# Seven products of quarters in place of the seventh product of blocks

## The chip, the cores and the metric

The kernel runs on one core of a Trainium2 chip. A core has a matrix engine (TensorE, PE in the profile; its weight loads are listed apart as PEld), two engines that work element by element (VectorE, DVE, and ScalarE, ACT), GpSimd (POOL), which here issues the DMAs that convert types, and SyncE (SP), which issues the other DMAs. Each engine works through its own instructions in order and waits at semaphores for the others. The metric is the time of one execution in microseconds (us), as the device measures it.

## The reference

The kernel computes a matrix product with a leaky ReLU behind it, all in 32-bit floats outside:

```python
m, k, n = 4096, 4096, 4096        # a: m x k, b: k x n, standard normal entries; alpha = 0.01
x = np.matmul(a, b)
return np.where(x > 0, x, alpha * x)
```

## The kernel before

**Blocks.** `out` is cut into 16 regions of 1024 rows by 1024 columns, (g, j) for row group g and column group j. The sum over k is cut into four units u of 1024 (eight slices of 128 each). Inputs are converted to 16-bit floats by the loading DMA. In a region, a is a 2x2 matrix of blocks (512 rows by 2048 of k), and so is b (2048 of k by 512 columns): b11 and b12 are units 0 and 1 with the left and the right columns, b21 and b22 units 2 and 3. Each block is held as two tiles k = 0, 1, one per unit. The pool of b (L73) has two buffers for each of the tags b11, b12, b21, b22, that is one block each: the next region's block goes where this region's block was, as soon as the last reader is done.

**Regions.** Region (0, 0) is computed directly, with 512 matmuls. The other 15 use Winograd's form of Strassen's scheme: seven products of blocks instead of eight, 64 matmuls of 128x128 weights by 512 columns each. `regions` (L480) has the order: (0,1) to (0,3), then for g = 1, 3 the columns 2, 0, 1, 3, and for g = 2 the columns 2, 0, 3, 1. The first of a group computes the sums of a's blocks (`sum_a`, named s1 to s4). The last of a group is called turning: while it runs, the next group's a is loaded by POOL through three buffers (`a16_pool`) and transposed by DVE (`fetch_a`, L660). The very last region, (3, 3), is called final. Column 2 is kept converted in DRAM, and regions (g, 2) load it through SP; all others load b through POOL.

**The seven products** (`PRODUCTS`, `product`, L617): 0 is a11*b11, 1 a12*b21, 2 s2*b11, 3 s3*b12, 4 s1*b11, 5 a22*b21, 6 s4*b22. The blocks of b are changed in place between them by DVE (`b_sum`): behind product 0, b12 becomes b22-b12 and b11 becomes b11+b12; behind product 1, b21 becomes b21-b11; behind product 2, b11 becomes b22-b11 with what b11 and b22 then are. b22 itself is product 6's operand. Products 0, 2, 4 and 6 accumulate in four PSUM banks y, products 1, and then 3 and 5, in the four others, z; the next region changes the two sets.

**Leaving.** `keep` copies the four banks to SBUF with ACT (u1 behind product 0, u2 behind product 2, v behind product 3). `add` adds banks onto such a copy with DVE, and `leave` applies the leaky ReLU with DVE and stores with SP. After product 6 the banks are copied, passed through the ReLU and stored (L748 to L754).

**The order.** The schedule is that of the program, written by hand: each engine executes its instructions in the order of the code. In a region's code the next region's blocks are fetched like this: b12 behind product 3 (L707), b11 behind product 4 (L728), b21 behind product 5 (L733), b22 behind product 6 (L747). A block is two units, a unit two DMAs of 512 KB on POOL's queue.

**Measuring.** The kernel sums squares of every block of a and b, and from these judges at the end (`judge`, L566) whether the scheme's result stands; otherwise a direct product follows (L757). One measure (`Measure`, L207): three squares by ACT (`begin`), one DVE addition, which frees a buffer for the fourth square, the fourth square, two more additions and a fold of some six small DVE instructions (`end`). `MEASURED` (L594) says which blocks are measured in which region and where: `middle` begins behind product 0, ahead of the copies of u1 on ACT, and ends behind the first b sums; the first of `late_ones` begins behind product 2 ahead of the copies of u2, the further ones behind product 3; `fifth` and `sixth` measure blocks that have been loaded for the next region.

Of the kernel before, what the change touches and what calls it, by code (L numbers as in the profile page):

```python
# [8 lines left out]
P = 128  # L9
DT = mybir.dt.float16  # L10
# [14 lines left out]
KC = 8  # L25
# [14 lines left out]
GREATEST = 1e8  # L40
# [4 lines left out]
def kernel(  # L45
# [6 lines left out]
):  # L52

# [20 lines left out]
    c_pool = ctx.enter_context(tc.tile_pool(name="c", bufs=8))  # L74
# [132 lines left out]
    class Measure:  # L207
# [21 lines left out]
        def end(self):  # L229
            total, *more = self.held  # L230
            nc.vector.tensor_add(total, total, more[0])  # L231
            self.square(3)
            nc.vector.tensor_add(total, total, more[1])  # L233
            nc.vector.tensor_add(total, total, self.held[3])  # L234
            fold(self.which, total, self.place(2), self.pairs)

# [246 lines left out]
    def fetch_b(i, quads):  # L483

        if i >= len(regions):
            return
        for half, nt in quads:
            for u in (2 * half, 2 * half + 1):
                fetch_unit(i, u, nt)
# [65 lines left out]
    def measure(i, which, x, y, room=None):  # L555

        if which:
            tiles = [have_b[i, 2 * x + k, y] for k in range(2)]
        else:
            tiles = [at[regions[i][0], x, 2 * y + k] for k in range(2)]  # L560
        parts = halves(tiles[0]) + halves(tiles[1])
        if tiles[0] is first_a:
            return MeasureFirst(which, parts, None)
        return Measure(which, parts, not which, room)

    def judge():  # L566
# [29 lines left out]
        (1, 2): (None, [A11], B12, B11), (1, 0): (B21, [B22, A12], B12, B11),  # L596
        (1, 1): (B21, [B22, A22], None, None),
        (2, 2): (None, [A11], None, None), (2, 0): (None, [A12], B12, B11),
        (2, 3): (B21, [B22, A22], None, None),
        (3, 2): (None, [A11], None, None), (3, 0): (A12, [A22], None, None),  # L600
    }

    PRODUCTS = [("a11", 0, 0), ("a12", 1, 0), ("s2", 0, 0), ("s3", 0, 1), ("s1", 0, 0), ("a22", 1, 0), ("s4", 1, 1)]

# [5 lines left out]
    for i, (g, j) in enumerate(regions):  # L610
# [19 lines left out]
        def keep(banks):  # L630
            kept = []
            for mt in range(MT):
                t = c_pool.tile([P, NT], FP32, name="c", tag="c")
                nc.scalar.copy(t, banks[mt])  # L634
                kept.append(t)
            return kept
# [34 lines left out]
        first_of_group = i == 0 or regions[i - 1][0] != g  # L671

# [3 lines left out]
        u1 = keep(y)  # L676
# [19 lines left out]
        u2 = keep(y)  # L696
# [9 lines left out]
        v = keep(z)  # L706
        fetch_b(i + 1, [(0, 1)])  # L707
        fetch_a(1, 0)
        for m in late_ones[1:]:
            m.begin()  # L710
            m.end()

        product(4, y, False)
        a21 = None
        if turning:
            new_s(g + 1, "s1")
            t = new_s(g + 1, "s2").rearrange("p k c m e -> p (k c m e)").bitcast(BF16)
            a21 = measure(i + 1, 0, 1, 0, t.rearrange("p (n w) -> p n w", n=4))
            a21.begin()
        add(v, y)  # L720
        leave(v, 1, 1)
        if a21:
            a21.end()
# [22 lines left out]
        product(6, y, False)  # L746
        fetch_b(i + 1, [(1, 1)])  # L747
        if final:  # L748
            even = nc.values_load(good[0:1, 0:1], min_val=0, max_val=1)
        for mt in range(MT):  # L750
            t = c_pool.tile([P, NT], FP32, name="c", tag="c")
            nc.scalar.copy(t, y[mt])  # L752
            leaky(t)
            nc.sync.dma_start(place(g, 0, mt, j, 1), t)  # L754


    with tc.If(even == 0):  # L757
        for m in range(M // RM):
# [9 lines left out]
            for n in range(N // NT):  # L768
# [12 lines left out]
                for mt in range(MT):  # L781
                    t = c_pool.tile([P, NT], FP32, name="c", tag="c")
                    nc.scalar.copy(t, banks[mt])
                    leaky(t)
                    nc.sync.dma_start(out[(m * MT + mt) * P:(m * MT + mt + 1) * P, cols], t)
# [35 lines left out]
```

## Time and profile before

| what | value |
| --- | --- |
| time, median of 3 runs | 1582.35 us (1581.85 to 1582.39) |
| the profiled execution, its own time | 1582.06 us |
| span of its instructions | 1580.2 us |
| granted TensorE clock, mean | 0.999 |
| PE busy | 1569.9 us (99%) |
| DVE busy | 956.8 us (61%) |
| ACT busy | 371.9 us (24%) |
| POOL busy | 306.5 us (19%) |
| casting DMA queue (POOL) | 141.59 MB, 60.2% of 16 engines' span |
| other DMA queue (SP) | 104.49 MB, 18.1% |

Times are microseconds, those of single instructions nanoseconds where marked ns. A line of the timeline has the start, the length, the engine, the line in the code, the operation with what it writes and reads, its shape and count, and in brackets the idle time before it with what ended that. A line of stages has the stretch from the span's start, its length, each engine's busy time with its count of instructions, then the granted clock, the DMA share and GB/s. A busy PE is not one at its peak, since matmuls overlap: what counts is the distance between their starts. A DMA share can be over 1, because the packets of an engine overlap.

### The profile page before, as it was taken

Reading aid. Unit: us, or ns where it says so; the run is one execution under the profiler, and the core shown is the slowest. Engines: PE = TensorE matmul, PEld = TensorE weight load, DVE = VectorE, ACT = ScalarE, POOL = GpSimd, SP = SyncE. Lnnn points to the kernel's source line nnn. Section 1 sums busy time; section 2 is a strip of 40 time slices with the busy share of each in tenths; the row PEclk is TensorE's granted clock in tenths of the full one; section 3 lists DMA queues with packets and bytes.
Section 4 is the critical chain, followed back from the end, with each engine's and each line's share of the span. In section 5 each row is a group of like instructions: output and inputs, shape, how many; then the busy total and the mean of one; then the engine's idle time right before and its main releaser. Section 6 shows DMA issues by size and latency. Waiting matters only on the chain.

```text
span 1580.2 us, 18237 instructions
## 1 busy us (share of the span) xinstructions
PE 1569.9 (99%) x7275; PEld 711.0 (45%) x7275; DVE 956.8 (61%) x1046; ACT 371.9 (24%) x390; POOL 306.5 (19%) x482
## 2 busy tenths in 40 slices
PE   9999999999999999999999999999999999999998
PEld 4444444444444444444444444444444444444443
DVE  4378758576876767647776464763878546351433
ACT  2201243302223364301221024431022122000110
POOL 5641110144002011124201102012520110201100
PEclk9999999999999999999999999999999999999999
DMA  9998795999539287499935919569993783938702
GB/s 244 187 215 180 161 281 144 198 189 210 203 72 204 72 146 148 82 215 163 268 124 103 217 32 181 134 89 225 169 256 114 111 183 65 201 80 142 152 27 83
DMA packets 216514, 247.74 MB, mean 157 GB/s; under 512 B 41057, under 2 KB 178529, under 8 KB 212322
## 3 DMA queue, kind: packets, MB, share of 16 engines
q0 software_dynamic: 173952, 141.59, 60.2%
q1 hardware_dynamic: 42178, 104.49, 18.1%
q8 instruction: 59, 0.97, 0.2%
q10 hardware_dynamic: 288, 0.39, 0.1%
q14 instruction: 37, 0.30, 0.1%
HBM read 310.38 MB, written 75.50 MB: 244 GB/s over the span
## 4 chain that ended last, share of the span: by engine, by line
PE 94%; DMA 4%; DVE 1%; issue 0%; POOL 0%; ACT 0%; SPq 0%; DVEq 0%
PE ps L625 92%; PE ps L274 2%; DMA b<-in_b_dram 2%; DMA a<-in_a_dram 1%; DVE a L136 1%; DMA a_in<-in_a_dram 0%; DVE part L313 0%; POOL a L127 0%; DVE part L309 0%; POOL b L184 0%; PE turned L361 0%; DVE a L368 0%; DVE c L302 0%; ACT c L752 0%; ACT a L368 0%
## 5 line engine op out<-in xcount | busy, mean ns | idle before, releaser
L625 PE MATMUL ps<-b,a 128*128 128x512 f16 x3840 | 836.1, 379 | 0.0
L625 PE MATMUL ps<-b,s 128*128 128x512 f16 x2880 | 628.9, 379 | 0.0
L625 PEld LDWEIGHTS <-a 128*128 128x128 f16 x3840 | 375.7, 98 | 453.1
L625 PEld LDWEIGHTS <-s 128*128 128x128 f16 x2880 | 281.8, 98 | 339.8
L500 POOL DMA_DIRECT2D b<-in_b_dram x184 | 136.7, 749 | 971.1 <-PE ps L625 646.9
L553 DVE TENSOR_TENSOR b<-b 128x4096 f16<-128x4096 f16 x112 | 253.4, 2290 | 100.9 <-DMA b<-in_b_dram 69.7
L640 DVE TENSOR_TENSOR c<-ps,c 128x512 f32<-128x512 f32 x180 | 111.7, 683 | 266.0 <-PE ps L625 189.5
L634 ACT COPY c<-ps 128x512 f32<-128x512 f32 x180 | 92.7, 600 | 607.4 <-PE ps L625 597.1
L302 DVE SCALAR_TENSOR_TENSOR c<-c 128x512 f32<-128x512 f32 x240 | 149.5, 686 | 77.3 <-ACT c L752 77.3
L127 POOL DMA_DIRECT2D a<-in_a_dram x252 | 143.9, 578 | 174.6 <-DVE a L136 103.5
L136 DVE STREAM_TRANSPOSE a<-a 128x512 uint32<-128x512 uint32 (+2 forms) x96 | 115.7, 1246 | 88.0 <-DMA a<-in_a_dram 87.9
L222 ACT ACTIVATE sq<-b 128x2048 bf16<-128x2048 f16 x64 | 119.4, 1913 | 107.0 <-DVE sq L231 93.1
L752 ACT COPY c<-ps 128x512 f32<-128x512 f32 x60 | 31.1, 600 | 364.6 <-PE ps L625 364.6
L274 PE MATMUL ps<-b,a 128*128 128x512 f16 x512 | 112.8, 379 | 1.8 <-DVE part L313 0.9
L222 ACT ACTIVATE sq<-a 128x2048 bf16<-128x2048 f16 x48 | 88.9, 1925 | 62.9 <-DVE sq L231 48.7
L274 PEld LDWEIGHTS <-a 128*128 128x128 f16 x512 | 49.6, 98 | 62.8 <-issue 3.1
L231 DVE TENSOR_TENSOR sq<-sq 128x2048 bf16<-128x2048 bf16 x27 | 33.0, 1222 | 32.2 <-ACT sq L222 32.2
L234 DVE TENSOR_TENSOR sq<-sq 128x2048 bf16<-128x2048 bf16 x27 | 33.1, 1225 | 17.2 <-ACT sq L222 17.2
L233 DVE TENSOR_TENSOR sq<-sq 128x2048 bf16<-128x2048 bf16 x27 | 33.1, 1226 | 4.7 <-ACT sq L222 2.3
L222 ACT ACTIVATE s<-a 128x2048 bf16<-128x2048 f16 x12 | 22.5, 1918 | 20.9 <-DVE a L136 20.9
L184 POOL DMA_DIRECT2D b<-in_b_dram x32 | 22.9, 726 | 6.1 <-DMA b<-in_b_dram 2.5
L240 DVE TENSOR_TENSOR sq<-sq 128x1024 bf16<-128x1024 bf16 x29 | 20.1, 692 | 1.0
(64 smaller groups left out, 256.2 us busy)
## 6 DMA issues: line engine op xcount, KB each, us to landing
b<-in_b_dram POOLq DMA_DIRECT2D x192, 512.0 KB, 8.3
out_dram<-c SPq DMA_DIRECT2D x240, 256.0 KB, 6.9
a<-in_a_dram POOLq DMA_DIRECT2D x244, 128.0 KB, 5.5
b<-kept SPq DMA_DIRECT2D x24, 1024.0 KB, 7.8
kept<-b SPq DMA_DIRECT2D x8, 1024.0 KB, 8.0
b<-in_b_dram POOLq DMA_DIRECT2D x24, 256.0 KB, 9.1
b_in<-in_b_dram SPq DMA_DIRECT2D x7, 512.0 KB, 7.7
out_dram<-part SPq DMA_DIRECT2D x4, 512.0 KB, 6.6
```

Of the source, the lines that this page charges most:

```text
L127: nc.gpsimd.dma_start(a16[32 * q:32 * q + 32], src.rearrange("(g i) w -> i g w", i=32))
L136: nc.vector.transpose(part.rearrange("p c m e -> p c (m e)").bitcast(U32) .rearrange("p c (g i) -> p g c i", i=32), src[:, :, i * n:(i + 1 ...
L222: nc.scalar.activation(to, self.parts[n], SQUARE)
L233: nc.vector.tensor_add(total, total, more[1])
L234: nc.vector.tensor_add(total, total, self.held[3])
L274: nc.tensor.matmul(ps, a_cols(at[0, h, u], c, mt, (h, u) == (0, 0)), bt[0, u, nt][:, c, :], start=first, stop=last,)
L302: nc.vector.scalar_tensor_tensor(t, t, alpha, t, op0=MULT, op1=MAX if alpha <= 1 else MIN)
L500: nc.gpsimd.dma_start(t[:, c:c + 4, :], b_rows(j, u, c, 4, nt))
L553: nc.vector.tensor_tensor(f(to), f(x0), f(x1), op)
L625: nc.tensor.matmul(banks[mt], a_cols(t, c, mt, t is first_a), B(half, nt, k)[:, c, :], start=first and (k, c) == (0, 0), stop=(k, c) == (1 ...
L634: nc.scalar.copy(t, banks[mt])
L640: nc.vector.tensor_add(acc[mt], banks[mt], acc[mt])
```

## The change

In nine regions (groups 1 to 3, neither turning nor final) product 6 is made by `quarters_product`. s4 and b22 are cut into 2x2 quarters (256 rows by 1024 of k, 1024 of k by 256 columns), and seven products of quarters replace the one product: 16 matmuls of 128 weights by 256 columns each, 112 in all. Four of them accumulate partly onto the banks y of product 4, the others in two banks that product 5 used. ACT copies and DVE additions combine them, and the sum with y leaves through `leave`.

The sums of s4's quarters (`sums_s4`) are made once a group, in its first region, and kept in DRAM (`kept_s`, 2 MB, four SP stores); the two other regions load them by SP behind product 4. The sums of b22's quarters (`sums_b`, four DVE instructions) are made in each of the nine regions. Their room is b12's two buffers and the three buffers of `a16_pool` (`rooms`). So b12 of the next region can't be loaded behind product 3 there: the four units of b22 and b12 are fetched behind the products of quarters, in the order in which their buffers come free.

b12 and b11 of the next region are then no longer measured ahead in the regions (1,2), (1,0) and (2,0). Instead `MeasureApart` reads the blocks of b once more, converted, into the measure's buffers by POOL, and squares them there: two such measures in (2,0), one in (3,0), three in (3,1). The copies for leaving become pairs of tiles with two tags c0 and c1 instead of one tag with eight buffers. The judge's upper limit is 1e7 instead of 1e8.

```diff
-    c_pool = ctx.enter_context(tc.tile_pool(name="c", bufs=8))
+    c_pool = ctx.enter_context(tc.tile_pool(name="c", bufs=2))
...
+    class MeasureApart(Measure):
+        def square(self, n):
+            to = self.place(n)
+            half, nt, jb = self.parts
+            nc.gpsimd.dma_start(
+                to.bitcast(DT).rearrange("p (c n) -> p c n", n=NT),
+                b_rows(jb, 2 * half + n // 2, n % 2 * 4, 4, nt))
+            nc.scalar.activation(to, to.bitcast(DT), SQUARE)
+            self.held.append(to)
...
-        (1, 2): (None, [A11], B12, B11), (1, 0): (B21, [B22, A12], B12, B11),
+        (1, 2): (None, [A11], None, None), (1, 0): (B21, [B22, A12], None, None),
         (1, 1): (B21, [B22, A22], None, None),
-        (2, 2): (None, [A11], None, None), (2, 0): (None, [A12], B12, B11),
+        (2, 2): (None, [A11], None, None), (2, 0): (B12 + (0,), [A12, B11 + (0,)], None, None),
         (2, 3): (B21, [B22, A22], None, None),
-        (3, 2): (None, [A11], None, None), (3, 0): (A12, [A22], None, None),
+        (3, 2): (None, [A11], None, None), (3, 0): (A12, [A22, B12 + (1,)], None, None),
+        (3, 1): (B11 + (1,), [B12 + (3,), B11 + (3,)], None, None),
...
+    def rooms(i):
+        two = [b_pool.tile([P, 2, KC * HALF], DT, name="q", tag="b12") for _ in range(2)]
+        three = [a16_pool.tile([P, KC * HALF], DT, name="sq4", tag="a16") for _ in range(3)]
+        tq = {2: two[0][:, 0], 1: two[0][:, 1], 4: two[1][:, 0]}
+        sq = {1: three[0], 2: three[1], 3: three[2], 4: two[1][:, 1]}
+        return tq, sq
...
+    def sums_b(i, tq):
+        y = quarters_b(i)
+        f = lambda n: tq[n].rearrange("p (c n) -> p c n", n=HALF)
+        tt = nc.vector.tensor_tensor
+        tt(y[0, 1], y[1, 1], y[0, 1], SUB)
+        tt(f(2), y[0, 1], y[0, 0], ADD)
+        tt(f(1), y[1, 1], f(2), SUB)
+        tt(f(4), y[1, 0], f(2), SUB)
+    def sums_s4(g, sq):
...
+        tt(f(1), x[1, 0], x[1, 1], ADD)
+        tt(f(2), f(1), x[0, 0], SUB)
+        tt(f(3), x[0, 0], x[1, 0], SUB)
+        tt(f(4), x[0, 1], f(2), SUB)
+        for n in range(4):
+            nc.sync.dma_start(kept_s[n], sq[n + 1])
...
+        def quarters_product(i, y, acc, other, tq, sq):
...
+            def part(xq, yq, to, first=False):
+                for c in range(KC):
+                    for m in range(2):
+                        rows = slice(m * P, (m + 1) * P)
+                        nc.tensor.matmul(
+                            to[m], xq[:, c // 2, rows, c % 2], yq[:, c, :],
+                            start=first and (c, m) == (0, 0), stop=c == KC - 1, skip_group_check=True,
+                        )
+            part(x[0, 1], b[1, 0], onto(0, 0))
+            part(x[0, 0], b[0, 0], into(acc), True)
+            nc.scalar.copy(block(0, 0), pair(acc))
+            part(quarter_a(sq[4]), b[1, 1], onto(0, 1))
+            part(quarter_a(sq[2]), f(2), into(acc))
+            nc.scalar.copy(block(0, 1), pair(acc))
+            part(quarter_a(sq[1]), f(1), into(other), True)
+            nc.vector.tensor_add(block(0, 1), pair(other), block(0, 1))
+            part(quarter_a(sq[3]), b[0, 1], into(acc))
+            for n in (1, 0):
+                nc.scalar.copy(block(1, n), pair(acc))
+            nc.vector.tensor_add(block(1, 1), pair(other), block(1, 1))
+            part(x[1, 1], f(4), onto(1, 0))
+            for mt in range(MT):
+                nc.vector.tensor_add(kept[mt], y[mt], kept[mt])
             return kept
...
+        in_quarters = g > 0 and not turning and not final
...
         product(3, z, True)
-        v = keep(z)
-        fetch_b(i + 1, [(0, 1)])
+        v = keep(z, side)
+        if not in_quarters:
+            fetch_b(i + 1, [(0, 1)])
         fetch_a(1, 0)
         for m in late_ones[1:]:
             m.begin()
             m.end()
+        if in_quarters:
+            tq, sq = rooms(i)
+            if first_of_group:
+                sums_s4(g, sq)
+                sums_b(i, tq)
         product(4, y, False)
...
         add(v, y)
         leave(v, 1, 1)
+        if in_quarters and not first_of_group:
+            for n in (4, 2, 1, 3):
+                nc.sync.dma_start(sq[n], kept_s[n - 1])
+            sums_b(i, tq)
...
-        product(6, y, False)
-        fetch_b(i + 1, [(1, 1)])
...
+        if in_quarters:
+            kept_c = quarters_product(i, y, new_bank(zbank + 2), new_bank(zbank + 3), tq, sq)
+            for u, nt in ((3, 1), (0, 1), (2, 1), (1, 1)):
+                fetch_unit(i + 1, u, nt)
+            leave(kept_c, 0, 1)
+            side = 1 - side
+        else:
+            product(6, y, False)
+            fetch_b(i + 1, [(1, 1)])
```

## The prediction

> R is the start of a region's product 0, T the start of its product 6; times behind them are us. A unit is half of a block of b (1 MB, two DMAs of 512 KB).
>
> **What bounds the kernel now.** I read the chain first.
>
> ```profile
> 122.86 1450.41 PE ps L625 x6720
> ```
>
> After 122.86 us it is matmuls alone: 215.8 ns each, 13.81 us a product, 96.7 us a region. A matmul saved there is time saved, and a wait put in is time lost. The PE timeline gives the pace of other widths and of a cold start:
>
> ```profile
> 1.19 4.88 PE L100 MATMUL wp<-w 128*128 128x512 f16 x11 [1.19 <-DVE x L86]
> ...
> 12.47 0.64 PE L361 MATMUL turned<-ident,a_rounded 128*128 128x128 f16 x8
> ...
> 689.05 13.98 PE L625 MATMUL ps<-b,s 128*128 128x512 f16 x64
> 702.86 27.79 PE L625 MATMUL ps<-b,a 128*128 128x512 f16 x128
> ```
>
> Eight of 128 columns, each with its own weights, take 0.64 us with the last one's 0.22 us: 60 ns apart. Next, stages (the last columns are granted clock, DMA share and GB/s): casting loads of b alone, two products before a region's end, and the end of the run.
>
> ```profile
> 112.00:122.00 10.00, 10.00 (x48) 4.48 (x47) 8.18 (x13) 0.00 (x0) 0.74 (x1) 1.00 1.24 206
> 689.05:702.86 13.81, 13.81 (x65) 6.27 (x64) 4.44 (x8) 0.45 (x1) 2.96 (x4) 1.00 1.17 226
> 1575.00:1577.00 2.00, 0.00 (x0) 0.00 (x0) 0.00 (x0) 0.00 (x0) 0.00 (x0) 1.00 0.38 139
> 1577.00:1578.00 1.00, 0.00 (x0) 0.00 (x0) 0.00 (x0) 0.00 (x0) 0.00 (x0) 0.51 0.03 8
> ```
>
> Backlogged casting loads move 206 GB/s, 5.1 us a unit, and around a region's end the DMA engines are already full. Last, DVE in the turning region (1,3), R = 702.86:
>
> ```profile
> 708.30 4.69 DVE L553 TENSOR_TENSOR b<-b 128x4096 f16<-128x4096 f16 x2 [2.77 <-DMA b<-in_b_dram]
> 716.39 4.69 DVE L553 TENSOR_TENSOR b<-b 128x4096 f16<-128x4096 f16 x2 [3.40 <-DMA b<-in_b_dram]
> 721.00 2.37 DVE L136 STREAM_TRANSPOSE a<-a 128x1024 uint32<-128x1024 uint32 x2
> ...
> 750.35 2.10 DVE L136 STREAM_TRANSPOSE a<-a 128x512 uint32<-128x512 uint32 x2 [3.75 <-DMA a<-in_a_dram]
> 752.37 4.45 DVE L553 TENSOR_TENSOR b<-b 128x4096 f16<-128x4096 f16 x2
> ```
>
> The first b sums wait for b22, with b12 long there. The last line makes product 4's operand: its first half is ready at 754.6, product 4 starts at 758.1. So there are 3.5 us of slack, and 2.9 in the next turning region, (2,1) (1141.9 against 1144.9). Durations come from the groups of the page and the list by line:
>
> ```profile
> L361 PEld LDWEIGHTS <-a_rounded 128*128 128x128 f16 x32 | 2.5, 120 | 2.4 <-DVE a_rounded L345 1.6 <-issue 0.6
> L640 DVE TENSOR_TENSOR c<-ps,c 128x512 f32<-128x512 f32 x180 | 111.7, 683 | 266.0 <-PE ps L625 189.5 <-issue 76.5
> L231 DVE TENSOR_TENSOR sq<-sq 128x2048 bf16<-128x2048 bf16 x27 | 33.0, 1222 | 32.2 <-ACT sq L222 32.2
> L222 ACT ACTIVATE sq<-b 128x2048 bf16<-128x2048 f16 x64 | 119.4, 1913 | 107.0 <-DVE sq L231 93.1 <-DVE sq L234 11.6 <-DMA b<-in_b_dram 2.3
> ```
>
> Their idle columns show the chain inside a measure (ACT's fourth square waits for DVE's first addition), which the change makes longer.
>
> **What PE gains.** Removed: 64 matmuls, 13.81 us. Added: 112 of 256 columns. Between 60 ns (128) and 215.8 ns (512) a line gives 112 ns; half of 215.8 is 108. I take 110: 12.3 us, a gain of 1.5 a region, 13.4 in nine (11.5 to 15.4).
>
> **Inside the product.** Part 2 (T+1.8) needs the third z bank, which the third of four additions L640 (2.48 us for four, from T-0.4) frees at T+1.4; the fourth is needed at T+7. ACT's copies (0.5 to 0.6 us) lie beside a 1.76 us part each. The last copies and the addition from the other bank end near T+12.1; the next product 0 wants these banks at T+12.7. Cost 0, if DVE is on time. The four sums of b's quarters are 128x2048 in 16 bits, as L231's 1.22 us: 4.9 us (9.2 if the strides cost the full rate of 2.3). They stand between product 4's leaving (its additions and leaky, 2.5 us each) and product 5's additions: done at T-4, 4 us of slack. The s4 sums (4.9 us, three times) end by R+69, before product 4 does: 0. The kept loads (2 MB, SP, issued T-8 behind v's stores, landing in some 7.8 us as the kept b did, sq4 first, wanted at T+3.5): 0, at most 2 in each of six regions. On SP, u2's stores stand behind these loads; u2's place is wanted only at the next R+14: 0.
>
> **What b12's move costs.** Before, b12 was loaded during products 3 and 4, at one unit per 6.9 us. Now four units go out when the seventh product's parts 3, 5, 6 and 7 are done, on POOL's queue behind b21, and the engines share with the kept loads and 2 MB of stores. Before, the second half of b22 was summed at R+13.5; two units more of 5.1 us put it at R+24, the first half, whole with the third unit, near R+19 (kept loads could add 0 to 5). The sums (4.6 us a half) end at R+24 and R+29; product 2 needs the halves at R+27.6 and R+34.5. In ordinary regions this fits, and the DVE work behind it is done before it is wanted (quarter sums at R+79, product 5's additions at R+83).
> It doesn't in the two turning regions that follow quarters, (1,3) and (2,1). Behind the b sums DVE has a's transposes, product 1's additions, the b21 sums, eight more transposes, then product 4's operand; POOL's a loads are queued behind b12 too, so their waits (1.4, 2.6, 3.8 us) move along. A shift of 10.3 less 3.5 and 2.9: PE waits 6.8 and 7.4 at product 4. **+14.2** (0 if the a waits close, 24 with the kept loads' 5).
>
> **What the moved measuring costs.** A measure that reads b again issues three POOL DMAs, then ACT squares (1.91 us each), a DVE addition that frees a buffer, a fourth DMA (5.4 us to land, the least among b's issues), a square, an addition and 2.7 us of folding. DVE waits through the fourth read, some 7 us that a measure on the chip doesn't have.
> (3,0), one late re-read: b sums end R+29.6; the middle measure of a on the chip takes 7.4 (1.2+1.9+1.2+3.0 folding), product 1's additions and leaky 5, four b sums 9.2, the first late measure 7.4: R+58.6. Buffers come free from R+55.6, the reads land R+61 to R+66, two squares and the addition R+66.8, the fourth read R+72.3, square, addition, fold R+78.2. Then product 4's additions and leaky 5, the quarter sums 4.9, the third z addition 1.9: R+90.0, where part 2 wants that bank at R+84.7: **5.4**.
> (2,0): its middle reads are behind b12: b whole at R+21 (5.1 a unit and 2.6 per MB of stores, added up from T) to R+24 (as above), the last read 7.7 later, its square 1.9, the first copy of u1, which stands behind the squares on ACT, 0.6: R+31 to R+34. Product 2 writes that bank at R+27.6: a wait of 3.6 to 6.6; I take 4, the rows for single durations being nearer. Late, as in (3,0): 5.4. **9.4**.
> (3,1): middle the same 4; two late re-reads, the second ending some 9 us later than (3,0)'s against a T 4 later: 10.5. **14.5**.
> The next region's b11 loads stand behind the re-reads on POOL and go out near R+70 to R+77 instead of R+63; they are wanted 20 us later: 0. Taken away are the fifth and sixth measures of (1,2), (1,0), (2,0), some 11 us of DVE each: beside PE before, worth 0. Together +29.3; below: 0, if the reads land 7 us sooner; above: 12 more, if the quarter sums cost 9.2.
>
> **The clock.** It was granted in full until 1577, 3.7 us after the last matmul (1573.3), then 0.51; and the first eleven matmuls took 425 ns apart, half speed for 4.9 us. Three of the waits (6.8, 7.4, 10.5) are longer than 3.7: 0 to 2.4 us each; I take 5 in all, towards the upper end because they exceed 3.7 clearly. The Trainium skill ("TensorE: Matmul & The Clock Gate", Part 1) states that an idle window of some 3.4 us halves the clock; the trace's end agrees, and no row of before shows a gap inside the run.
>
> **Sum**, against the profiled run's 1582.06 (span 1580.2; the median of runs is 1582.35, 0.3 above): -13.4 +14.2 +29.3 +5 = +35: 1617.
>
> **Rivals.**
> Earlier landing (other side): if DMA absorbs the two units in idle time and b12 is complete at R+17 instead of R+24, turning regions don't wait, (2,0) and (3,0) don't, (3,1) keeps 3.5: 1582.1-13.4+3.5 = 1572. It decides at about R+19, where the waits sum to 13.4. For it: DMA is nearly idle from R+14 to R+41, and share above 1 counts overlapping packets. Against: 206 and 226 GB/s at the very place. 0.20.
> Only the measured regions wait, because a's transposes catch up: 1582.1-13.4+29.3+2 = 1600; 0.11. Only the turning ones, the measures being ready in time: 1582.1-13.4+14.2+3 = 1586; 0.07.
> Weight loads set the pace of narrow matmuls. For it: the row of the transposes has 120 ns for a load, more than 110. Against: those loads overlapped, as 60 ns apart shows. At 120 ns the seventh product takes 13.4 us, the gain is 3.3 in all: 1617+10 = 1627; from 123 ns on nothing is gained. 0.06. The Trainium skill (same page, Back-to-back issue gap) speaks for it: a stream of pairs of weight load and matmul is paced by both, about 81 ns at 128 columns against 56 for a matmul alone. The trace's 60 ns disagrees. With the page's 25 ns on top, an estimate for 256 columns is 134 ns, and the sum would be 1641.
> Quarter sums at the full 2.3 us each: the three late regions wait 4 more: 1617+12 = 1629; 0.05.
> The change does not do what it says: if the lowered limit 1e7 sent the work to the other path, the time would be far off; sums of some 1000 squares of standard normals stay near 1000. Under 0.01.
>
> **Numbers.** The likeliest has 0.51; its own range is 1600 to 1631. Range 1571 to 1631: it leaves out somewhat under half of the earlier-landing case and what lies above the sum (longer waits with the kept loads' 5). 0.2% is 3.2 us, about what can be told from none. Faster 0.20 (earlier landing); same 0.04 (the turning-only case reaches it in half of its width); slower 0.76.
>
> **What would show it.** Matmuls of 128x256 about 110 ns apart; PE idle ahead of product 4 in (1,3) and (2,1), ended by a DVE b sum; ahead of product 2 in (2,0) and (3,1), ended by an ACT copy behind squares; ahead of part 2 in (2,0), (3,0), (3,1), ended by DVE's additions; granted clock below 1 behind the longest; b sums starting near R+19 and R+24. Wrong would be: b sums at R+17 or before, a spacing over 123 ns, or PE without gaps.

## The result and the profile after

| | before | after |
| --- | --- | --- |
| time, median | 1582.1 us (1581.25 to 1582.39) | 1654.57 us (1652.07 to 1655.53) |
| the profiled execution / its span | 1582.06 / 1580.2 us | 1655.53 / 1653.6 us |
| granted TensorE clock, mean | 0.999 | 0.978 |

The ratio is 1.0457 (95%: 1.0438 to 1.0475): 72.5 us slower. The prediction was 1617, 35 slower, with the range 1571 to 1631. The sign was right, and the time lies above the range.

The view that says most is the list of PE's waits of the changed kernel (who waits, at which line, for whom; us in all, times, longest). These are the six largest groups that belong to the regions (two of 0.2 us for kept sums are left out); before, the chain of matmuls had none there.

```profile
PE ps L714 <- DVE c L738: 19.7, 5, 8.4
PE ps L683 <- ACT c L696: 15.6, 2, 8.4
PE ps L683 <- DVE b L566: 15.5, 5, 7.7
PE ps L683 <- ACT c L868: 5.0, 2, 3.2
PE ps L683 <- DVE c L738: 3.1, 5, 2.2
...
PE ps L683 <- DMA a<-in_a_dram: 1.4, 1, 1.4
```

L714 is the matmuls of quarters, L683 those of blocks, L738 the additions of `add`, L696 the copies of `keep`, L566 the sums of b, L868 the copies behind an undivided product 6. The same waits in the PE timeline show their places, and what stands in the regions between them:

```profile
237.19 1.07 PE L683 MATMUL ps<-b,a 128*128 128x512 f16 x2 [3.23 <-ACT c L868]
240.05 15.24 PE L683 MATMUL ps<-b,a 128*128 128x512 f16 x62 [1.79 <-ACT c L868]
...
503.76 3.66 PE L714 MATMUL ps<-b,s 128*128 128x256 f16 x32
...
774.10 16.56 PE L683 MATMUL ps<-b,s 128*128 128x512 f16 x64 [6.48 <-DVE b L566]
...
948.29 16.59 PE L683 MATMUL ps<-b,s 128*128 128x512 f16 x64 [7.27 <-ACT c L696]
...
1011.79 3.39 PE L714 MATMUL ps<-b,s 128*128 128x256 f16 x16 [3.73 <-DVE c L738]
...
1187.91 16.16 PE L683 MATMUL ps<-b,s 128*128 128x512 f16 x64 [7.71 <-DVE b L566]
...
1418.13 3.31 PE L714 MATMUL ps<-b,s 128*128 128x256 f16 x16 [6.70 <-DVE c L738]
...
1467.38 16.45 PE L683 MATMUL ps<-b,s 128*128 128x512 f16 x64 [8.36 <-ACT c L696]
...
1536.57 3.57 PE L714 MATMUL ps<-b,s 128*128 128x256 f16 x16 [8.39 <-DVE c L738]
```

Two things are to be seen. The line at 503.76 is parts 1 and 2 of a product of quarters in a region without waits: 32 matmuls in 3.66 us. And the lines behind a wait are long themselves. A product of 64 matmuls takes 13.98 us by such a line before, 13.81 from start to start; the four that follow waits of 6.5 to 8.4 us take 16.2 to 16.6, and a part of 16, 1.9 us by such a line elsewhere, takes 3.3 to 3.6. So a wait costs more than its own length. The stages of the same kernel (stretch, length, busy PE, PEld, DVE, ACT and POOL, then granted clock, DMA share, GB/s), behind two of these waits:

```profile
948.00:958.00 10.00, 9.71 (x33) 3.65 (x33) 4.63 (x8) 6.13 (x7) 0.00 (x0) 0.73 0.35 52
1536.00:1545.00 9.00, 8.18 (x54) 5.79 (x54) 3.52 (x6) 1.17 (x2) 1.48 (x2) 0.75 1.11 325
```

PE is busy nearly throughout the first of them, at a mean clock of 0.73, and makes 33 matmuls, where 10 us at 215.8 ns hold 46. Before, the clock stood at 1.00 from the first region to the end.

From the starts of the products in the two PE timelines each region's length follows. A region takes 96.7 us without quarters, and with quarters 95.1 where nothing waits ((1,2), (1,0), (2,2), (2,3), (3,2)). What the others take beyond that is split here into the waits, which the lists give, and the rest, which is matmuls made more slowly. (A wait is counted from the end of a matmul, 379 ns behind its start, and without it the next start would come after 215.8; so some 0.16 us of each of the 22 waits, 3.6 us in all, is in the last column.)

| region | length | beyond 96.7 or 95.1 | waits | slower matmuls |
| --- | --- | --- | --- | --- |
| (0,2) | 104.2 | 7.5 | 5.0 | 2.5 |
| (1,1) | 96.0 | 0.9 | 0.5 | 0.4 |
| (1,3), turning | 111.0 | 14.3 | 9.2 | 5.1 |
| (2,0) | 111.5 | 16.4 | 11.2 | 5.2 |
| (2,1), turning | 111.7 | 15.0 | 10.3 | 4.7 |
| (3,0) | 104.6 | 9.5 | 6.9 | 2.6 |
| (3,1) | 118.6 | 23.5 | 17.6 | 5.9 |
| sum | | 87.1 | 60.7 | 26.4 |

Less nine gains of 1.59 us, 14.3, this is +72.8, which is the difference of the two spans (73.4) but for 0.6 ahead of the regions.

The loads and the sums of b, first before and then after (DMA rows: KB each, median us from issue to landing; group rows: busy, mean ns, idle before it and what ended that):

```profile
b<-in_b_dram POOLq DMA_DIRECT2D x192, 512.0 KB, 8.3
...
L553 DVE TENSOR_TENSOR b<-b 128x4096 f16<-128x4096 f16 x112 | 253.4, 2290 | 100.9 <-DMA b<-in_b_dram 69.7
```

```profile
b<-in_b_dram POOLq DMA_DIRECT2D x192, 512.0 KB, 15.0
...
sq<-kept_s SPq DMA_DIRECT2D x18, 512.0 KB, 12.4
...
L566 DVE TENSOR_TENSOR b<-b 128x4096 f16<-128x4096 f16 x112 | 252.8, 2290 | 165.7 <-DMA b<-in_b_dram 156.9
```

The casting loads of b land in 15.0 us for 8.3, and DVE's sums wait 156.9 us for b, where they waited 69.7.

### The profile page after: what moved, and what is told of

Same layout as the page of the kernel before. It is cut to its first block, busy times and chain, and to the rows that moved or that the text cites. A ratio compares the mean times of both kernels' runs of the same rounds, so it can differ in the third digit from the quotient of the medians.

```text
span 1653.6 us, 19247 instructions
## 1 busy us (share of the span) xinstructions
PE 1580.3 (96%) x7707; PEld 756.7 (46%) x7707; DVE 1044.9 (63%) x1148; ACT 374.2 (23%) x390; POOL 324.2 (20%) x506
## 5 line engine op out<-in xcount | busy, mean ns | idle before, releaser
L683 PE MATMUL ps<-b,a 128*128 128x512 f16 x3840 | 842.8, 381 | 9.6 <-ACT c L868 5.0
L683 PEld LDWEIGHTS <-a 128*128 128x128 f16 x3840 | 376.6, 98 | 466.8 <-issue 19.6
L683 PE MATMUL ps<-b,s 128*128 128x512 f16 x2304 | 513.0, 384 | 31.1 <-ACT c L696 15.6
L683 PEld LDWEIGHTS <-s 128*128 128x128 f16 x2304 | 227.1, 99 | 312.4 <-issue 29.4
L566 DVE TENSOR_TENSOR b<-b 128x4096 f16<-128x4096 f16 x112 | 252.8, 2290 | 165.7 <-DMA b<-in_b_dram 156.9
L513 POOL DMA_DIRECT2D b<-in_b_dram x184 | 136.6, 748 | 806.9 <-PE ps L683 553.4
L696 ACT COPY c<-ps 128x512 f32<-128x512 f32 x180 | 92.2, 598 | 473.8 <-PE ps L683 395.6
L738 DVE TENSOR_TENSOR c<-ps,c 128x512 f32<-128x512 f32 x180 | 111.6, 683 | 128.1 <-PE ps L683 86.5
L287 PE MATMUL ps<-b,a 128*128 128x512 f16 x512 | 112.9, 379 | 2.2 <-DMA b<-in_b_dram 0.9
L223 ACT ACTIVATE sq<-a 128x2048 bf16<-128x2048 f16 x48 | 88.8, 1921 | 88.0 <-DVE sq L232 72.5
L223 ACT ACTIVATE sq<-b 128x2048 bf16<-128x2048 f16 x40 | 74.4, 1910 | 106.8 <-DVE sq L232 98.3
L287 PEld LDWEIGHTS <-a 128*128 128x128 f16 x512 | 49.7, 98 | 63.2 <-issue 3.3
L247 ACT ACTIVATE sq<-sq 128x2048 bf16<-128x2048 f16 x24 | 45.8, 1910 | 113.6 <-DMA sq<-in_b_dram 84.4
L232 DVE TENSOR_TENSOR sq<-sq 128x2048 bf16<-128x2048 bf16 x27 | 33.0, 1224 | 46.3 <-ACT sq L247 30.1
L235 DVE TENSOR_TENSOR sq<-sq 128x2048 bf16<-128x2048 bf16 x27 | 33.1, 1225 | 44.6 <-ACT sq L247 31.7
L714 PEld LDWEIGHTS <-s 128*128 128x128 f16 x432 | 44.3, 103 | 29.6 <-issue 20.6
L244 POOL DMA_DIRECT2D sq<-in_b_dram x24 | 17.8, 743 | 201.6 <-DVE sq L235 97.5
L714 PE MATMUL ps<-b,s 128*128 128x256 f16 x288 | 38.1, 294 | 19.7 <-DVE c L738 19.7
L721 ACT COPY c<-ps 128x512 f32<-128x512 f32 x9 | 5.3, 586 | 212.0 <-PE ps L714 212.0
## 6 DMA issues: line engine op xcount, KB each, us to landing
sq<-kept_s SPq DMA_DIRECT2D x18, 512.0 KB, 12.4
```

Of the source, the lines that this page charges most:

```text
L223: nc.scalar.activation(to, self.parts[n], SQUARE)
L247: nc.scalar.activation(to, to.bitcast(DT), SQUARE)
L287: nc.tensor.matmul(ps, a_cols(at[0, h, u], c, mt, (h, u) == (0, 0)), bt[0, u, nt][:, c, :], start=first, stop=last,)
L513: nc.gpsimd.dma_start(t[:, c:c + 4, :], b_rows(j, u, c, 4, nt))
L566: nc.vector.tensor_tensor(f(to), f(x0), f(x1), op)
L683: nc.tensor.matmul(banks[mt], a_cols(t, c, mt, t is first_a), B(half, nt, k)[:, c, :], start=first and (k, c) == (0, 0), stop=(k, c) == (1 ...
```

## The experiments

All times of this section are to be read against 1581.8 to 1582.3 for the kernel before and 1654.57 for the changed one, whose four runs lie 3.5 us apart. A time without a range behind it is that of one execution.

### Taking the re-reads away

```diff
-        (2, 2): (None, [A11], None, None), (2, 0): (B12 + (0,), [A12, B11 + (0,)], None, None),
+        (2, 2): (None, [A11], None, None), (2, 0): (None, [A12], None, None),
...
-        (3, 2): (None, [A11], None, None), (3, 0): (A12, [A22, B12 + (1,)], None, None),
+        (3, 2): (None, [A11], None, None), (3, 0): (A12, [A22], None, None),
-        (3, 1): (B11 + (1,), [B12 + (3,), B11 + (3,)], None, None),
```

> The changed kernel without the six measures that read b again (their sums of squares are left out, so the judge sees fewer blocks). Late-load theory: (2,0), (3,0) and (3,1), 111.5, 104.6 and 118.6 us long, lose 16, 9 and 23 us and become 95 to 96; (1,3) and (2,1) stay near 111: about 1655 - 48 = 1606 to 1608. Rival (b12's lateness alone holds these regions up, the re-reads only come on top): they keep half of it, 1625 to 1635.

1605.22 us. (2,0) and (3,0) fall to 95.1, (3,1) to 95.5; (1,3), (2,1) and (0,2) keep 111.2, 110.2 and 103.0. So these six measures, with their reads, squares and folds, are the cause of 49.4 us, nearly all of it in these three regions.

### The place that the last copies take

In (0,2) the wait has nothing to do with the later load of b12. The changed kernel's ACT timeline and its SP queue there:

```profile
236.55 1.07 ACT L868 COPY c<-ps 128x512 f32<-128x512 f32 x2 [22.86 <-DMA out_dram<-c]
```

```profile
201.72 24.99 SPq L515 DMA_DIRECT2D kept<-b  x4
226.80 2.01 SPq L743 DMA_DIRECT2D out_dram<-c  x4
```

In a region without quarters, L866 takes the last copies' tiles with `new_c(1 - side)`, and those are the places of u2. U2's stores (L743) are behind the stores of kept b on SP's queue, which wait for b21 to land, so that u2's stores leave SP only from 226.8 on. Product 1 of (0,2) then finds the banks of (0,1)'s product 6 still full. Undone:

```diff
-            side = 1 - side
         else:
...
-            _, kept_c = new_c(1 - side)
+            _, kept_c = new_c(side)
...
+        side = 1 - side
```

> The changed kernel, but in regions without quarters the last copies take the places of v (as the pool of eight gave them) instead of those of u2, and the two sides change in every region. Theory of the places: (0,2), 104.2 us long with product 1 waiting for these copies, becomes 96.7, all else the same: 1647. Rival (the wait there is a late store queue that any place would meet, since SP sends u2's stores only behind the kept b): no change, 1655.

1648.76 us, and (0,2) is 96.7. The copies go ahead at once; its ACT timeline:

```profile
219.62 2.05 ACT L867 COPY c<-ps 128x512 f32<-128x512 f32 x4 [5.84 <-PE ps L683]
```

That settles this term: 7.5 us by the region, 5.8 by the whole time.

### Quarters not ahead of the turning regions

```diff
-        in_quarters = g > 0 and not turning and not final
+        in_quarters = g > 0 and not turning and not final and (g, j) not in [(1, 1), (2, 3)]
```

> The changed kernel with quarters in seven regions: not in (1,1) and (2,3), which stand before the turning ones. Late-load theory: (1,3) and (2,1), 111.0 and 111.7 us, fall to 96.7 each, (2,3) and (1,1) rise to 96.7: 1655 - 29.3 + 2.3 = 1628. Rival (turning regions wait because of what the change does to SP, the copies or the clock, not because b12 comes late): they stay above 105, 1640 to 1658.

1631.63 us. (1,3) and (2,1) fall to 96.7, as they must if what waits in them is the b that quarters made late. (1,1) takes 97.8 and (2,3) is back to a plain product. (2,0) grew from 111.5 to 114.3, with waits of 7.60 and 5.11 for 7.27 and 3.73; why wasn't followed, and this is most of the distance to the expected 1628.

### Late loads without quarters

Product 6 stays in one piece and the sums of quarters and the kept loads go; what is left of the change is b12 fetched behind it, and the measuring.

```diff
-            kept_c = quarters_product(i, y, new_bank(zbank + 2), new_bank(zbank + 3), tq, sq)
-            for u, nt in ((3, 1), (0, 1), (2, 1), (1, 1)):
+            product(6, y, False)
+            for u, nt in ((2, 1), (0, 1), (3, 1), (1, 1)):
                 fetch_unit(i + 1, u, nt)
+            _, kept_c = new_c(side)
+            for mt in range(MT):
+                nc.scalar.copy(kept_c[mt], y[mt])
             leave(kept_c, 0, 1)
...
-        if in_quarters:
-            tq, sq = rooms(i)
...
-            for n in (4, 2, 1, 3):
-                nc.sync.dma_start(sq[n], kept_s[n - 1])
-            sums_b(i, tq)
```

> Product 6 in one piece as before, no sums of quarters, nothing kept in DRAM; b12 fetched behind it all the same, and the re-reads as in the change. If the late order of the loads makes the waits, they stay: 1655 + 14 of lost gain, less what the 2 MB of kept loads cost in lateness. If those 2 MB cost 4 to 5 us, the first b sums start near R+19 and R+24 instead of R+23.4 and R+28.6, waits in five places are 4 us shorter, and the time is near 1650. If they cost nothing, b sums stay near R+22 and R+27 and the time is 1665 to 1670. Rival (the quarters themselves make the waits): waits vanish except the re-reads', 1615 to 1630.

1628.36 us, below both numbers of the late-load theory, since the run also lacks what the part-2 waits need: product 6 asks for no z bank, and no quarter sums stand on DVE. (3,0), which had only that wait, is 96.7. The time lies in the rival's range (1615 to 1630), but not by the rival's reason: the turning regions still wait, (1,3) 6.5 us and (2,1) 6.9. The units are fetched in another order here, so that the first half of b is whole with the second of them; the second half needs the fourth, as in the change. DVE's b sums in (1,3) (R = 710.27):

```profile
723.20 4.69 DVE L566 TENSOR_TENSOR b<-b 128x4096 f16<-128x4096 f16 x2 [10.27 <-DMA b<-in_b_dram]
734.02 4.69 DVE L566 TENSOR_TENSOR b<-b 128x4096 f16<-128x4096 f16 x2 [6.13 <-DMA b<-in_b_dram]
```

and its product 4 on PE:

```profile
772.18 15.30 PE L683 MATMUL ps<-b,s 128*128 128x512 f16 x64 [6.50 <-DVE b L566]
```

The second half is summed from R+23.8, against R+13.5 before: 10.3 us, two units of 5.1. Of that shift 6.5 us arrive at PE, where the prediction's chain gave 6.8. In the changed kernel the same sums start at R+23.4 and R+28.6, each with the kept loads beside b:

```profile
730.48 4.68 DVE L566 TENSOR_TENSOR b<-b 128x4096 f16<-128x4096 f16 x2 [18.84 <-DMA b<-in_b_dram]
735.69 4.69 DVE L566 TENSOR_TENSOR b<-b 128x4096 f16<-128x4096 f16 x2 [0.53 <-DMA a<-in_a_dram]
```

So the rest of the lateness, some 5 us on the second half, is the quarters' own: the kept loads, or the moment at which the parts let the buffers go. The next run bears on which.

### The kept sums loaded earlier

```diff
         if in_quarters:
             tq, sq = rooms(i)
             if first_of_group:
                 sums_s4(g, sq)
                 sums_b(i, tq)
+            else:
+                for n in (4, 2, 1, 3):
+                    nc.sync.dma_start(sq[n], kept_s[n - 1])
...
         if in_quarters and not first_of_group:
-            for n in (4, 2, 1, 3):
-                nc.sync.dma_start(sq[n], kept_s[n - 1])
             sums_b(i, tq)
```

> The changed kernel, but the 2 MB of kept sums are loaded behind product 3, when the DMA is idle, and not behind product 4's leaving. Theory (they delay b by 4.6 us where they are): b sums in (1,1) and (1,3) start at R+19 and R+24 again, (1,1) loses its wait, (1,3) and (2,1) get 4 to 8 us shorter, (2,0) and (3,0) don't change, (3,1) little (its forerunner's loads still come behind a re-read): 1638 to 1643. Rival (2 MB cost the same wherever they are): 1655.

1646.39 us, between the two forecasts. DVE's sums of b in (1,1) (R = 611.85):

```profile
632.97 4.67 DVE L566 TENSOR_TENSOR b<-b 128x4096 f16<-128x4096 f16 x2 [16.56 <-DMA b<-in_b_dram]
638.14 4.69 DVE L566 TENSOR_TENSOR b<-b 128x4096 f16<-128x4096 f16 x2 [0.51 <-DMA b<-in_b_dram]
```

They start at R+21.1 and R+26.3, for R+23.6 and R+28.7 in the changed kernel. (1,3) falls from 111.0 to 106.4, (2,1) from 111.7 to 107.7, and (1,1) to 95.1. Loaded a product earlier, the 2 MB give back 2.4 us of lateness. Regions whose predecessor loads no kept sums start them at R+19.3 to R+20, so one to two more us stay; what takes those wasn't settled.

### Copies ahead of the re-read's squares

The waits ahead of product 2 in (2,0) and (3,1) end with ACT's copies, which stand behind the squares of the middle re-read. Is that order the cause, or the re-read's length?

```diff
-        if middle:
+        if middle and not isinstance(middle, MeasureApart):
             middle.begin()
         u1 = keep(y, side)
+        if isinstance(middle, MeasureApart):
+            middle.begin()
```

> The changed kernel, but in (2,0) and (3,1) ACT copies u1 before the squares of the middle re-read. The waits of 7.4 and 8.5 us ahead of product 2 go. If these copies are the cause of that time, (2,0) and (3,1) get some 10 us shorter each: 1635. If DVE's chain (middle fold, late folds, quarter sums, product 5's additions) is the limit of the region, it ends where it did and the wait ahead of part 2 grows by what was saved, less one spell of half clock: (2,0) near 109, (3,1) near 116: 1650.

1654.15 us, no change, and nearest to the second forecast: (2,0) takes 112.0, (3,1) 118.1. The wait moved. In (2,0) (R = 912.68), PE timeline:

```profile
957.68 0.38 PE L683 MATMUL ps<-b,a 128*128 128x512 f16 x1 [3.40 <-DVE c L738]
...
1011.43 3.26 PE L714 MATMUL ps<-b,s 128*128 128x256 f16 x16 [7.57 <-DVE c L738]
```

The 7.27 us ahead of product 2 are gone, and in their place stand 3.40 ahead of product 3 and 7.57, for 3.73, ahead of part 2, both ended by DVE's additions. DVE works in order, and the re-read holds it: in the changed kernel it sat 5.2 us for the fourth square in the middle of the region and 5.1 in the late measure (5.15 and 5.36 in this run):

```profile
954.22 1.23 DVE L235 TENSOR_TENSOR sq<-sq 128x2048 bf16<-128x2048 bf16 x1 [5.20 <-ACT sq L247]
...
996.36 1.23 DVE L235 TENSOR_TENSOR sq<-sq 128x2048 bf16<-128x2048 bf16 x1 [5.13 <-ACT sq L247]
```

### What a wait costs beside itself

The kernel before, with squares that nobody reads put on ACT ahead of the copies of u1 in six regions. That holds back product 2 by a chosen time, with nothing else of the change.

```diff
+        for wide in HOLD.get((g, j), []):
+            to = a16_pool.tile([P, 2048], BF16, name="hold", tag="a16")
+            nc.scalar.activation(to[:, :wide], halves(at[g, 0, 0])[0][:, :wide], SQUARE)
         u1 = keep(y)
```

> The kernel before, with added squares on ACT (into a buffer nobody reads) ahead of the copies of u1 in six regions, so that product 2 waits there for about 1.5 us in (1,2), 2.3 in (2,2), 3.3 in (2,0), 4.2 in (3,2), 6.0 in (3,1), 9.7 in (3,3): 27 us of waits. It measures what a wait costs beyond itself. If each wait of 2 us or more is followed by matmuls at half clock that lose some 2.4 us, the time is 1582 + 27 + 12 = 1621; if only waits over 3.7 us are, 1616; if none are, 1609.

1612.75 us. The waits came out at 20.6 us in all and not at 27, so the three totals can't be compared with it as they stand; the products behind the waits can. The six products 2 in the PE timeline:

```profile
440.88 14.79 PE L628 MATMUL ps<-b,s 128*128 128x512 f16 x64 [0.47 <-ACT c L637]
829.95 14.79 PE L628 MATMUL ps<-b,s 128*128 128x512 f16 x64 [1.32 <-ACT c L637]
929.89 14.79 PE L628 MATMUL ps<-b,s 128*128 128x512 f16 x64 [2.27 <-ACT c L637]
1224.07 16.48 PE L628 MATMUL ps<-b,s 128*128 128x512 f16 x64 [3.12 <-ACT c L637]
1425.04 16.79 PE L628 MATMUL ps<-b,s 128*128 128x512 f16 x64 [4.92 <-ACT c L637]
1533.23 15.62 PE L628 MATMUL ps<-b,s 128*128 128x512 f16 x64 [8.52 <-ACT c L637]
```

A plain product has 13.98 in such a line. After a wait of 0.47 to 2.27 us it has 14.79: 0.8 more at full clock, whatever the wait. That it is the same 0.8 fits four banks which come free one after another at the pace of ACT's copies. After 3.12 us and more the clock is below 1, and the product loses 0.8 to 2.0 us on top.

By this run alone a limit would lie between 2.3 and 3.1 us, but the changed kernel's trace shows that the length of a wait isn't what decides. Its clock also fell behind the waits of 2.20 us in (1,3) and 1.43 us in (2,1). Inside its regions it has ten spells at half clock, which last 3.41, 6.83 or 10.24 us and start a whole number of 3.41 us apart. So the stretches to look at are those of 3.41 us between such moments. Those around the waits of 2.27 and 3.12 us of this run, counted from its clock's fall at 1225.79 (PE's busy time stands first, the granted clock third from the end):

```profile
925.42:928.83 3.41, 2.20 (x11) 0.88 (x9) 0.00 (x0) 3.41 (x3) 0.00 (x0) 1.00 0.00 0
928.83:932.24 3.41, 2.02 (x8) 0.70 (x8) 2.37 (x4) 3.41 (x6) 0.00 (x0) 1.00 0.00 0
932.24:935.66 3.42, 3.42 (x17) 1.52 (x16) 3.42 (x6) 3.42 (x3) 0.00 (x0) 1.00 0.54 204
...
1222.38:1225.79 3.41, 1.39 (x5) 0.43 (x5) 1.74 (x3) 3.41 (x6) 0.00 (x0) 1.00 0.00 0
1225.79:1229.20 3.41, 3.41 (x10) 1.22 (x9) 3.41 (x4) 3.41 (x3) 0.00 (x0) 0.50 0.01 2
```

and those around the 2.20 and the 1.43 us of the changed kernel, with the sum of its ten spells:

```profile
748.62:752.03 3.41, 0.99 (x5) 0.31 (x4) 3.27 (x4) 2.06 (x4) 1.50 (x3) 1.00 1.14 173
752.03:755.44 3.41, 3.38 (x8) 1.02 (x8) 3.41 (x6) 0.00 (x0) 1.19 (x3) 0.50 1.12 171
...
1161.63:1165.04 3.41, 1.53 (x6) 0.39 (x4) 3.41 (x5) 1.98 (x4) 1.69 (x4) 1.00 1.14 176
1165.04:1168.45 3.41, 3.19 (x9) 1.14 (x8) 3.41 (x6) 0.00 (x0) 0.47 (x1) 0.50 1.23 200
...
sum 68.27, PE 40.52 PEld 16.64 DVE 46.73 ACT 21.99 POOL 9.88; mean PE 4.05 PEld 1.66 DVE 4.67 ACT 2.20 POOL 0.99
```

Stretches in which PE was busy for 0.99, 1.39 and 1.53 us are followed by one at half clock, those with 2.02 and 2.20 us are not. The 2.27 us lie across two stretches and leave enough work in both; the 1.43 us lie in one, together with the short gaps behind them. This is read off the traces, and no run was made for it. The Trainium skill ("TensorE: Matmul & The Clock Gate", Part 1) puts the return to half clock at an idle window of some 3.4 us. Here a stretch of that length which was idle for a little over half of it was already enough.

### Quarters with the measures on the chip

If the waits come from re-reads, turning regions and the place of the copies, quarters in six regions without these should keep their gain. b12 and b11 are measured as before, ahead, in regions whose own product 6 is undivided.

```diff
-        in_quarters = g > 0 and not turning and not final
+        QUARTERED = [(1, 2), (1, 0), (2, 2), (2, 0), (3, 0), (3, 1)]
+        in_quarters = (g, j) in QUARTERED
...
-        (1, 1): (B21, [B22, A22], None, None),
+        (1, 1): (B21, [B22, A22], B12, B11),
...
-        (2, 3): (B21, [B22, A22], None, None),
-        (3, 2): (None, [A11], None, None), (3, 0): (A12, [A22, B12 + (1,)], None, None),
-        (3, 1): (B11 + (1,), [B12 + (3,), B11 + (3,)], None, None),
+        (2, 3): (B21, [B22, A22], B12, B11),
+        (3, 2): (None, [A11], B12, B11), (3, 0): (A12, [A22], None, None),
```

with (2,0)'s entry as in the first experiment and the copies' places as in the second.

> Quarters in six regions, (1,2), (1,0), (2,2), (2,0), (3,0), (3,1); (1,1), (2,3) and (3,2) keep product 6 in one piece and load b12 early, so the next region's b12 and b11 are measured there on the chip, and nothing reads b again; the places of the copies as in the run with its own side. Late-load theory: no long wait is left: 1582.2 - 6 x 1.59 = 1572.7, plus at most 2 us for half a microsecond here and there ahead of product 2 where kept loads make b late: 1573 to 1575, faster by 0.5 to 0.6%. Rival (a part of the waits has a cause not seen yet): 1578 or more.

1575.38 us (1574.53 to 1578.26), ratio 0.9962 (0.9948 to 0.9976): faster than the kernel before by some 6 us. Six gains of 1.59 are 9.5, and 1.8 us of waits for b are left, with slower matmuls behind them.

### A seventh region, three ways

(3,2) in quarters too. Then column 0's b12 and b11 can't be measured ahead and must be read again somewhere. First as the late measures of the final region:

```diff
+QUARTERED = [..., (3, 2), ...]
-        (3, 2): (None, [A11], B12, B11), (3, 0): (A12, [A22], None, None),
+        (3, 2): (None, [A11], None, None), (3, 0): (A12, [A22], None, None),
+        (3, 3): (None, [B12 + (0,), B11 + (0,)], None, None),
```

> As the six, with quarters in (3,2) too; the two blocks that (3,2) measured ahead are read again in (3,3), both as late measures, where DVE has no quarter sums behind them and no a to transpose. Theory: another 1.6 gained, the reads land in (3,3)'s idle DMA time, the second fold ends near R+79, product 4's additions near R+81.5, product 6 wants them at R+82.9: 1571 to 1574. Rival (two re-reads are too much there as well, and the judge behind them ends after the last product): 1575 to 1585.

1579.59 us, 0.9985 (0.9976 to 0.9994). The rival's number was right, and nearly its reason. The final region has no room behind it: the last fold of the measures ends near 1551.3, and then the judge's chain runs on DVE, which the last copies and stores wait for.

```profile
1550.99 0.34 DVE L268 TENSOR_TENSOR stats<-stats,r 128x16 f32<-128x16 f32 x3
...
1561.36 0.59 DVE L594 TENSOR_REDUCE most<-line 1x2 f32<-1x256 f32 x1 [4.93 <-DMA line<-lines]
...
1564.40 0.15 DVE L601 TENSOR_TENSOR good<-ok 1x1 int32<-1x1 f32 x1
```

The chain ends 2.3 us ahead of the last matmul (1566.9), not behind it, but product 5's additions and eight passes of the ReLU still stand behind it on DVE. In the kernel before it ended at 1557.6, 15.7 us ahead of the last matmul. From the last matmul to the end of the span it is now 12.4 us for 6.9.

So the two re-reads go to the middle of (2,2) and (3,2), the first regions of their groups, which had no middle measure:

```diff
+        (2, 2): (B12 + (0,), [A11], None, None),
+        (3, 2): (B11 + (0,), [A11], None, None),
-        (3, 3): (None, [B12 + (0,), B11 + (0,)], None, None),
```

> Quarters in seven regions ((1,1) and (2,3) left out), column 0's b12 and b11 read again as middle measures in (2,2) and (3,2), where b itself comes by SP, the POOL queue is empty and DVE idles ahead of product 1's end; nothing in (3,3). Theory: 1582 - 7 x 1.59 = 1570.9 plus 2 to 3 us ahead of product 2 behind kept loads: 1573 to 1574. Rival (DVE is full in the first region of a group, with s3, s4 and their quarter sums): part 2 waits there, 1578 or more.

1575.01 us, 0.9958 (0.9944 to 0.9971). The list of waits has one group left in the regions, for b:

```profile
PE ps L683 <- DVE b L566: 1.9, 4, 0.8
```

These waits are what early kept loads took away from (1,1) above. So the third version has both: e10 with the kept loads behind product 3.

> The same, with the kept sums loaded behind product 3. Theory: the half microseconds ahead of product 2 go as well: 1571 to 1572. Rival (these waits have another cause): as the run before.

1572.07 us (1570.71 to 1573.54), 0.9936 (0.9923 to 0.995). It is faster than both kernels. Its list of PE's waits has only groups of the start (L374, L287, L101, before the first region of the scheme), and its page reads:

```profile
PE 1558.9 (99%) x7611; PEld 744.3 (47%) x7611; DVE 1027.4 (65%) x1128; ACT 372.7 (24%) x390; POOL 312.3 (20%) x490
...
sq<-kept_s SPq DMA_DIRECT2D x12, 512.0 KB, 4.7
```

Seven regions take 95.1 to 95.2 us, and no other more than before. The kept loads land in 4.7 us, for 12.4 in the changed kernel. Seven gains of 1.59 are 11.1; some 10 were measured, and in the profiled execution, one of 1573.54 us, the rest is lost ahead of the first region, which starts at 125.2 for 122.7. So a product of quarters is worth what the prediction counted for it; the changed kernel loses it to what was moved and put around it.

## Why the prediction was right and wrong

The places of the waits were right and the sizes too small. The step that failed most is the clock's: the prediction let it be lost only behind waits of over 3.7 us, three of them, at 5 us in all. The prediction's sum against the same terms as measured (the waits of the table, and slower matmuls in a row of their own):

| term | predicted | measured |
| --- | --- | --- |
| gain of PE, nine products | -13.4 | -14.3 |
| turning regions (1,3) and (2,1), waits | 14.2 | 19.5 |
| measuring: (2,0), (3,0), (3,1), waits | 29.3 | 35.6 |
| clock (measured: all matmuls made more slowly) | 5 | 26.4 |
| kept loads at "0, at most 2 in each of six regions": (1,1)'s wait | 0 | 0.5 |
| the copies' places: (0,2)'s waits | not counted | 5.0 |
| sum | +35 | +72.7 |

**Gain of PE: right.** 110 ns a matmul was taken; 32 matmuls in 3.66 us with the last one's length are 109.2 ns apart, a product 12.23 us, the gain 1.59 for 1.5. The rival by weight loads fell. So did the number that the Trainium skill ("TensorE: Matmul & The Clock Gate", Back-to-back issue gap) would give, estimated at 134 ns for such a stream: the row says 109.2.

**Inside the product: right.** No wait where DVE is on time (five regions of 95.1), and the quarter sums ran at 1.22 to 1.23 us, not at the 2.3 of the rival.

**b12's move: place, chain and releaser right, size low.** PE waits ahead of product 4 in both turning regions, for a b sum. Alone, without quarters, the move gave 6.5 us where 6.8 was forecast. The step that failed is "kept loads could add 0 to 5", of which 0 was taken: they landed in 12.4 us, not 7.8, and in (1,1), (1,3) and (2,1) b sums behind them start at R+23.4 to R+28.8, for R+19 and R+24. (In (2,3), (3,1) and (3,3), behind regions that themselves wait in the seventh product, they start at R+20.8 to R+26.4.) Behind regions without kept loads they started at R+19.3 to R+25.2, as forecast. 9.2 and 10.3 us of waits came for 6.8 and 7.4, spread over products 2 to 4.

**Measuring: right in places and releasers, low by a fifth.** All five waits are where they were expected, for an ACT copy behind squares ahead of product 2 in (2,0) and (3,1), and for DVE's additions ahead of part 2 in all three. 7.27 and 8.36 stand for the 4 of the middle, 3.73, 6.70 and 8.39 for the late 5.4, 5.4 and 10.5. The middle's range was 3.6 to 6.6, and the low end was chosen because "the rows for single durations" were nearer; b was whole later than either end had it. When the copies were put ahead of the squares, the wait went elsewhere: what binds there is DVE's order with its two halts of 5 us, and not ACT's.

**The clock: the worst-sized term.** The prediction took from the end of the run that only waits over 3.7 us lose the clock, found three, and counted 5 us. That row gave no limit: it fits a stretch of 3.41 us which began 0.3 us behind the last matmul and was idle throughout. The changed kernel has ten spells at half clock, eight at waits of 3.2 us and more and two behind waits of 2.20 and 1.43 us. PE was busy for 40.5 us inside them; half of that, some 20 us, is an estimate of what the clock took. The rest of the 26.4 is the 3.6 us that are waits by another count, and banks that come one by one, for which the prediction had no term (0.8 us a wait where the copies were held); these weren't parted for each wait. 21.4 of the missing 37.5 us are in this row.

**The copies' places: not seen.** The diff's pool line and `new_c(1 - side)` were described, but no price was given to which place a tile gets, and so whose store is waited for. 5.0 us of waits, 7.5 with what follows them.

**The rivals.** "Earlier landing", the one that ended on the other side, fell: its own point of decision was R+19, and no half came before that in a region behind quarters. "Only the measured regions" and "only the turning ones" fell too, since each of the two kinds waits when the other's cause is taken away. The rivals were put side by side as alternatives; none of them let the sum grow in every term at once, and so the range ended 24 us short.

## What to carry to other kernels

When a change lends a buffer out, the load that wanted it is moved, and so is every load behind it on the same queue; the price is read at the engine that needs the last of them, along that engine's own order, and the slack there (here 3 us) decides. A wait put into a stream of matmuls is to be counted with what it does to the matmuls behind it, here 0.8 us for a short one and up to 2.8 in all for a long one. And where a change has a gain and a cost in different regions, do it only in the regions that have the slack: seven products of quarters instead of nine, with their measures in regions that have room, turn +72.5 us into -10.

## What the runs showed of the hardware

- The granted clock fell in steps of 3.41 us: a stretch of that length in which PE was busy for 0.99 to 1.53 us was followed by one at half clock, and one with 2.02 or 2.20 us was not. So a wait of 1.43 us could cost the clock and one of 2.27 us not. Behind a wait of 3.12 us the product took 16.48 us for 14.79. A longer wait does not cost more in the matmuls: behind 8.52 us the product took 15.62.
- Matmuls of 128x256, each with weights of its own, keep 109.2 ns from start to start, just over half the 215.8 of 128x512; their weight loads, 98 to 103 ns each by the groups of L714, don't lengthen that distance.
- 2 MB of plain loads on SP's queue, issued beside 4 MB of casting loads on POOL's, landed in 12.4 us, and in three regions the sums of what the casting loads brought started some 4 us later than behind regions without them. Issued a product earlier they landed in 7.8 us and gave back 2.4 of those 4; in the fastest version, which issues them there, they land in 4.7.
